# Where the kept weight tiles of a decoder trunk's block products are loaded, and who forms their first sum

## The chip, the cores and the metric

The kernel runs on one core of a Trainium2 chip. The metric is the device time of one execution in microseconds (us). Four compute engines of the core matter here: TensorE (PE in the profile; PEld is its weight load), VectorE (DVE), ScalarE (ACT) and GpSimd (POOL). SyncE (SP) issues the plain loads; POOL issues the accumulating ones. Each engine works through its own list of instructions in order.

## The reference

Two layers of a decoder trunk on 256 positions of width 1024, in float32. Each layer is a half-step feed-forward network (FFN), a token mixer, and a second FFN; the four FFNs are alike. The part that the change touches is the FFN:

```
def swiglu(x, w_in, w_out):
    gate, up = jnp.split(x @ w_in, 2, axis=-1)
    return (jax.nn.silu(gate) * up) @ w_out
...
h = h + 0.5 * swiglu(rms_norm(h, ffn1_norm[l]), ffn1_w_in[l], ffn1_w_out[l])
```

`w_in` is 1024 x 5632 and `w_out` 2816 x 1024. The mixer is a Mamba-2 branch and a gated DeltaNet branch, merged.

## The kernel before, in words

**Weights stream once.** All weights lie in DRAM as tiles of 128 x 1024 float32 (512 KB), in the order of use. A tile is loaded (`load`, L167) and then split on the chip into two float32r halves (`prep`, L180): ScalarE rounds it to `whi` and VectorE subtracts, `wlo = w - whi`. Each product takes three matmuls (`mm3`, `mm3w`, L320 to L332). Raw tiles (`wraw`) have 5 buffers (`NRAW`), the halves 5 pairs (`NSPL`). `take` (L206) hands the next split tile to TensorE and, ahead of that, loads up to `limit` and splits up to 5 forms further on. So a plain load waits on SyncE until VectorE is done with the tile that held its buffer, and a split waits until TensorE is done with the one that held its halves.

**The order of an FFN** is the string `FFN` (L36): one `f` (4 tiles), twenty `c` (2 tiles of `w_in` each, 48 matmuls of 128x256), and in between four `A`; then the close, `BdBBBddddd`. An `A` and its `B` compute one 2x2 block product of `w_out` in Strassen-Winograd form: four weight blocks b11, b12, b21, b22 (two row pairs side by side, 512 KB each) and seven products instead of eight. The weight operands of an `A` are b11, b11+b12, b12+b22 and b11+b12+b22, those of a `B` are b22, b21 and b11+b12+b21+b22. The six `d` tiles are plain rows of `w_out`. The close goes over into the next stage's normalisation: the residual is added to `h`, ScalarE and VectorE normalise, and TensorE transposes the result (`hnT`, L286), first for one half of the positions, then for the other. `join` (L421) adds four combined results to `h` with accumulating transfers.

**A kept tile** (`wsum`, four buffers y0 to y3) carries the sums of one `A` until its `B`. `plan_ffn` (L106) lists the transfers (`stream`) and the forms (`plan`). Two places of `FFN` ahead of each `A` it lists b11 into the kept tile (kind `y`, SyncE) and b12 added onto it by POOL (kind `+`, `add_to`, L164). At the `A` it lists three plain tiles: b12, b22 and again b11. Form `q1` splits the kept b11+b12, and VectorE forms b12+b22 in b12's tile; `q0` splits the plain b11, and VectorE adds b22 onto the kept tile; `q2` splits b12+b22; `q3` splits the kept b11+b12+b22, and then POOL adds b21 onto it (L196), for `q6` in the `B`.

**Who decides the order.** The instructions of one engine are not issued in the order of the source: a scheduler places them by their dependences, and `tc.issue_after` pins one behind another. A plain load waits for one of five buffers. A kept tile has its own buffer, free since the `B` of four groups earlier, and nothing pins its load.

Of the kernel before, what the change touches and what calls it, by code (L numbers as in the profile page):

```python
# [52 lines left out]
def trunk_kernel(ctx, tc, x, wst, wsm, norms, lpar, rpar, cst, out):  # L53
# [15 lines left out]
    def tt(o, a, b, op):  # L69
        return V.tensor_tensor(out=o, in0=a, in1=b, op=op)  # L70
# [15 lines left out]
    def trb(name):  # L86
        return trp.tile([P, 512], F32, tag="tr", name=name)
# [18 lines left out]
    def plan_ffn(j):  # L106


        o, j2, begun, held = j + 4 * FC, j + 4 * FC + 22, [], []
        spots, q = [], 0  # L110
        for at, kind in enumerate(FFN):
            if kind == "A":
                spots.append(at - 2)
        o1 = o + FFN[: FFN.index("A")].count("d")
        for at, kind in enumerate(FFN):
            if at in spots:
                y = len(stream)
                stream.extend([("y", o1 + 4 * q), ("+", o1 + 4 * q + 1, y)])
                begun.append(y)
                q += 1  # L120
            if kind in "fc":
                j = plan_plain(j, 4 if kind == "f" else 2)
            elif kind == "d":
                o = plan_plain(o, 1)
            elif kind == "A":
                y, u = begun.pop(0), len(stream)
                stream.extend([("w", o + 1), ("w", o + 2), ("w", o)])
                plan.append(("q1", (y, u, u + 1), u + 2))
                plan.append(("q0", (u + 2, y, u + 1), u + 3))
                plan.append(("q2", (u,), u + 3))  # L130
                plan.append(("q3", (y, o + 3), u + 3))
                held.append((y, o + 2))
                o += 4
            else:
                y, b22 = held.pop(0)
                stream.append(("w", b22))
                plan.append(("q4", (len(stream) - 1,), len(stream)))
                stream.append(("w", b22 + 1))
                plan.append(("q5", (len(stream) - 1,), len(stream)))
                plan.append(("q6", (y,), len(stream)))  # L140
        return j2
# [19 lines left out]
    def tile_of(i):  # L161
        return wst[i // 2, :, (i % 2) * 1024 :][:, 0:1024]
# [4 lines left out]
    def load(j):  # L167
        kind, i = stream[j][:2]
        if kind == "+":
            add_to(raws[stream[j][2]], i)  # L170
            return
        if kind == "y":
            r = slots.tile([P, 1024], F32, tag=f"y{state['first']}", name="wsum")
            state["first"] = (state["first"] + 1) % 4
        else:
            r = wpool.tile([P, 1024], F32, tag="wraw", name="wraw", bufs=NRAW)
        state["last"] = nc.sync.dma_start(r[:], tile_of(i))
        raws[j] = r

    def prep(i):  # L180
        kind, js, _ = plan[i]
        hi = wpool.tile([P, 1024], F32R, tag="whi", name="whi", bufs=NSPL)
        lo = wpool.tile([P, 1024], F32R, tag="wlo", name="wlo", bufs=NSPL)
        r = raws[js[0]]
        with ExitStack() as behind:
            for ins in state["behind"].pop(i, ()):
                behind.enter_context(tc.issue_after(ins))
            act(hi[:], r[:])
            if kind in ("q0", "q1"):
                to, by = (raws[k][:] for k in js[1:])  # L190
                tt(to, to, by, ALU.add)
            if i in state["late"]:
                behind.enter_context(tc.issue_after(state["late"].pop(i).ins))
            tt(lo[:], r[:], f(hi[:]), ALU.subtract)
        if kind == "q3":
            add_to(r, js[1])  # L196
        for k in {"q0": (js[0], js[-1]), "q1": (), "q3": ()}.get(kind, (js[0],)):
            raws.pop(k)
        halves[i] = (hi, lo)

# [265 lines left out]
    def ffn(nxt):  # L466
        gh = [slots.tile([P, 8, S], F32R, tag=t_, name="gh") for t_ in ("sA", "sB", "sC")]
        gl = [slots.tile([P, 8, S], F32R, tag=t_, name="gl") for t_ in ("sD", "sE", "sF")]

        bsa = slots.tile([P, 2, 2, 3, P], F32R, tag="sG", name="bsa")  # L470
        bsb = slots.tile([P, 16, P], F32R, tag="sH", name="bsb")
        bsc = slots.tile([P, 4, 2, P], F32R, tag="sI", name="bsc")
        bsd = s2.tile([P, 2, 2, P], F32R, tag="s2", name="bsd")
        bsb3 = bsb[:, 0:12].rearrange("p (i o j) t -> p i o j t", i=2, o=2)
        bsb1 = bsb[:, 12:16].rearrange("p (i o) t -> p i o t", i=2)

        def sums(p, j):

            q, i = (p - 1) // 2, (p - 1) % 2
            if j < 3:  # L480
                b = (bsa[:], bsb3)[q % 2]
                return b[:, i, 0, j, :], b[:, i, 1, j, :]
            b = (bsc[:, 0:2], bsc[:, 2:4], bsb1, bsd[:])[q]
            return b[:, i, 0, :], b[:, i, 1, :]

        def block_sums(p, g2):

            sf = tmp2("sf")
            a11, a21, a12, a22 = (g2[:, j * P : (j + 1) * P] for j in range(4))
# [24 lines left out]
        tok_chunk(ps, range(KT))  # L514
        gt = []
        for t in range(2):
            sg = tmp2("sg")
            act(sg[:, 0:256], ps[t][:, 0:256], AF.Silu)
            tt(sg[:, 256:512], sg[:, 0:256], ps[t][:, 256:512], ALU.mult)
            gt.append(sg[:, 256:512])  # L520
        todo, pb, n, cut = FFN[1:], {}, 0, False
        for c in range(FC - 1):
            g2 = tmp2("g2")
            for a in range(2):
                ps = accb("fc")
                chan_chunk(ps, cut or (c, a) == (1, 0))
                cut = False
                sg = s2.tile([P, S], F32, tag="ca", name="sg", bufs=2)
                act(sg[:], ps[:, 0:S], AF.Silu)
                tt(g2[:, a * S : (a + 1) * S], sg[:], ps[:, S : 2 * S], ALU.mult)  # L530
                todo = todo[1:]
                if c == 0 and a == 0:
                    bank = trb("gT")
                    for k in range(2):
                        for t in range(2):
                            PE.transpose(bank[:, k * S + t * P : k * S + (t + 1) * P], gt[t][:, k * P : (k + 1) * P], ident)
                    split(0, bank[:].rearrange("p (k t) -> p k t", k=2))
            split(2 * c + 2, g2[:].rearrange("p (k t) -> p k t", k=2))
            if c + 1 <= PAIRS[-1][-1]:
                block_sums(c + 1, g2)  # L540
            if todo[0] == "A":
                if not pb:
                    pb.update({i: trb(f"p{i}") for i in (5, 6, 1, 7)})
                four = [
                    (pb[5], lambda p: sums(p, 0), PAIRS[n]),
                    (pb[1], lambda p: stat(2 * p, 0), PAIRS[n]),
                    (pb[7], lambda p: sums(p, 2), PAIRS[n]),
                    (pb[6], lambda p: sums(p, 1), PAIRS[n]),
                ]
                block_products(four, n == 0, n == len(PAIRS) - 1)  # L550
                todo, cut = todo[1:], True
                n += 1
        po = [[accb("o"), accb("o")] for _ in range(2)]

        return close_blocks(po, stat, sums, pb, nxt)
# [841 lines left out]
```

## Time and profile before

| what | us |
|---|---|
| median of 3 runs (lowest, highest) | 1556.36 (1554.48, 1556.77) |
| the profiled execution | 1555.2 |
| its span, first to last instruction | 1553.4 |
| TensorE busy in it | 1529.5 |
| VectorE busy | 1210.0 |
| ScalarE busy | 945.9 |
| GpSimd busy | 100.7 |

The page names groups by line, engine, operation and tile. Times within the span count from its start. A matmul's busy time overlaps the next one's, so the distance from one start to the next says how fast TensorE goes: in the FFN's `c` stages 0.11 us from one 128x256 matmul to the next, in the close 0.23 us from one 128x512 matmul to the next. The rows that carry the argument stand in the prediction.

### The profile page before, as it was taken

The numbers are of one execution on the slowest core, as the hardware profiler recorded it, in microseconds if no ns is written. First come the engines' busy times: TensorE is split into PE (matmuls) and PEld (weight loads), VectorE is DVE, ScalarE is ACT, GpSimd is POOL, SyncE is SP. The second block draws the span as 40 slices with busy tenths as digits, with TensorE's granted clock in tenths as the row PEclk, the third lists the DMA queues.
The fourth block names the chain that finished last, engine by engine and source line by source line (L and its number), as shares of the span: only waits on it lengthen the run. The fifth ranks groups of instructions, "written<-read, shape, count | busy, mean of one in ns | idle before, by whom it ended". The sixth has DMA issues, their size and how long they took to land.

```text
span 1553.4 us, 29029 instructions
## 1 busy us (share of the span) xinstructions
PE 1529.5 (98%) x11458; PEld 1384.0 (89%) x11458; DVE 1210.0 (78%) x1840; ACT 945.9 (61%) x1534; POOL 100.7 (6%) x108
## 2 busy tenths in 40 slices
PE   8999999999999999999899999999999999999998
PEld 7999889999888888999689998899998888889996
DVE  6778768967899766878677787699579996677786
ACT  5555677765576545655455566676756665455564
POOL 0000110000000000000100011000000000000010
PEclk9999999999999999999999999999999999999999
DMA  8878775653564686678967787666446557856785
GB/s 292 262 244 261 229 224 165 190 158 109 192 202 163 212 239 200 180 241 248 313 199 209 219 258 231 206 187 187 124 126 213 178 165 223 245 179 199 226 250 156
DMA packets 103439, 322.50 MB, mean 208 GB/s; under 512 B 23350, under 2 KB 24326, under 8 KB 102279
## 3 DMA queue, kind: packets, MB, share of 16 engines
q1 hardware_dynamic: 96390, 299.68, 58.4%
q0 software_dynamic: 6912, 20.97, 8.0%
q8 instruction: 90, 1.47, 0.4%
q14 instruction: 47, 0.38, 0.1%
HBM read 314.50 MB, written 1.92 MB: 204 GB/s over the span
## 4 chain that ended last, share of the span: by engine, by line
PE 82%; DVE 6%; DMA 4%; issue 3%; ACT 3%; POOL 1%; SPq 0%; POOLq 0%; ACTq 0%; DVEq 0%
PE fc L332 9%; PE fc L326 9%; PE fc L331 9%; PE t L321 3%; PE t L322 3%; PE t L323 3%; DMA wraw<-in_wst_dram 3%; PE b L323 3%; PE b L321 3%; PE b L322 3%; PE o L323 2%; PE o L322 2%; PE o L321 2%; DVE wlo L70 2%; PE p L322 2%
## 5 line engine op out<-in xcount | busy, mean ns | idle before, releaser
L70 DVE TENSOR_TENSOR wlo<-wraw,whi 128x1024 fp32r<-128x1024 f32 x504 | 611.2, 1220 | 171.6 <-ACT whi L67 159.9
L67 ACT ACTIVATE whi<-wraw 128x1024 fp32r<-128x1024 f32 x504 | 527.7, 1058 | 275.8 <-PE fc L331 76.6
L332 PE MATMUL fc<-uW,wlo 128*128 128x256 f32 x1280 | 354.8, 277 | 0.0
L326 PE MATMUL fc<-uW,whi 128*128 128x256 f32 x1280 | 354.1, 277 | 0.0
L331 PE MATMUL fc<-uW,whi 128*128 128x256 f32 x1260 | 348.2, 276 | 0.0
L326 PEld LDWEIGHTS fc<-uW,whi 128*128 128x128 f32 x1280 | 240.3, 188 | 0.8
L332 PEld LDWEIGHTS fc<-uW,wlo 128*128 128x128 f32 x1280 | 240.5, 188 | 0.0
L331 PEld LDWEIGHTS fc<-uW,whi 128*128 128x128 f32 x1260 | 236.5, 188 | 0.8
L321 PE MATMUL t<-whi,uW 128*128 128x512 f32 x256 | 101.9, 399 | 0.0
L322 PE MATMUL t<-wlo,uW 128*128 128x512 f32 x256 | 100.9, 394 | 0.0
L323 PE MATMUL t<-whi,uW 128*128 128x512 f32 x256 | 100.6, 393 | 0.0
L321 PE MATMUL b<-whi,bh 128*128 128x512 f32 x192 | 76.2, 398 | 0.3 <-ACT bh L67 0.2
L322 PE MATMUL b<-wlo,bh 128*128 128x512 f32 x192 | 75.0, 390 | 0.0
L323 PE MATMUL b<-whi,bl 128*128 128x512 f32 x192 | 74.3, 394 | 0.3 <-DVE bl L70 0.3
L326 PE MATMUL xs<-uW,whi 128*128 128x256 f32 x256 | 72.7, 284 | 0.0
L332 PE MATMUL xs<-uW,wlo 128*128 128x256 f32 x256 | 71.3, 278 | 0.0
L331 PE MATMUL xs<-uW,whi 128*128 128x256 f32 x254 | 70.5, 277 | 0.0
L67 ACT ACTIVATE whi<-wsum 128x1024 fp32r<-128x1024 f32 x48 | 50.8, 1058 | 27.8 <-PE fc L331 23.3
L70 DVE TENSOR_TENSOR wlo<-wsum,whi 128x1024 fp32r<-128x1024 f32 x48 | 58.6, 1221 | 11.4 <-ACT whi L67 10.4
L322 PE MATMUL o<-wlo,gh 128*128 128x512 f32 x160 | 63.9, 399 | 2.5 <-DVE wlo L70 2.5
L321 PE MATMUL o<-whi,gh 128*128 128x512 f32 x160 | 63.9, 399 | 2.4 <-ACT whi L67 2.4
L165 POOL DMA_DIRECT2D wsum<-in_wst_dram x32 | 28.1, 878 | 582.3 <-DVE wlo L70 464.4
(332 smaller groups left out, 3430.4 us busy)
## 6 DMA issues: line engine op xcount, KB each, us to landing
wraw<-in_wst_dram SPq DMA_DIRECT2D x520, 512.0 KB, 5.0
wsum<-in_wst_dram POOLq DMA_DIRECT2D x32, 512.0 KB, 8.2
wsum<-in_wst_dram SPq DMA_DIRECT2D x16, 512.0 KB, 7.9
dc<-rdram SPq DMA_DIRECT2D x8, 1024.0 KB, 8.4
nw<-in_norms_dram SPq DMA_DIRECT2D x6, 512.0 KB, 6.8
h<-u POOLq DMA_DIRECT2D x12, 256.0 KB, 8.0
gb<-rdram SPq DMA_DIRECT2D x8, 256.0 KB, 5.7
h<-in_x_dram SPq DMA_DIRECT2D x4, 256.0 KB, 3.2
```

Of the source, the lines that this page charges most:

```text
L67: return A.activation(out=o, in_=i, func=func, **kw)
L70: return V.tensor_tensor(out=o, in0=a, in1=b, op=op)
L165: G.dma_start(out=r[:], in_=tile_of(i), accum_op=ALU.add)
L321: PE.matmul(ps, lh, rh, start=start, stop=False)
L322: PE.matmul(ps, lh, rl, start=False, stop=False)
L323: return PE.matmul(ps, ll, rh, start=False, stop=stop)
L326: PE.matmul(ps, wh, mh, start=start, stop=False)
L331: PE.matmul(ps, wh, ml, start=False, stop=False)
L332: PE.matmul(ps, wl, mh, start=False, stop=stop)
```

## The change

Three things change. The kept tile's b11 is listed at its `A`, no longer two places ahead, and its load is issued behind the load listed ahead of it (`issue_after`). b11 is loaded once, into the kept tile only, and VectorE forms b11+b12 there from the plain b12; the accumulating transfer of b12 is gone. The forms come in the order b11, b11+b12, b12+b22, b11+b12+b22 (`q0`, `q1`, `q2`, `q3`), and so do the four products and their result banks (`pb`). Accumulating transfers still form the sum of all four blocks.

Per `A`: SyncE's loads go from four (b11, b12, b22, b11) to three, POOL's accumulating ones from two (b12, b21) to one (b21), VectorE's 128x1024 sums from two to three. There are 16 `A`.

```diff
             elif kind == "A":
-                y, u = begun.pop(0), len(stream)
-                stream.extend([("w", o + 1), ("w", o + 2), ("w", o)])
-                plan.append(("q1", (y, u, u + 1), u + 2))
-                plan.append(("q0", (u + 2, y, u + 1), u + 3))
-                plan.append(("q2", (u,), u + 3))
-                plan.append(("q3", (y, o + 3), u + 3))
+                y = len(stream)
+                stream.extend([("y", o), ("w", o + 1), ("w", o + 2)])
+                plan.append(("q0", (y, y, y + 1), y + 2))
+                plan.append(("q1", (y, y + 1, y + 2), y + 3))
+                plan.append(("q2", (y + 1, y, y + 2), y + 3))
+                plan.append(("q3", (y, o + 3), y + 3))
...
-        state["last"] = nc.sync.dma_start(r[:], tile_of(i))
+        with ExitStack() as behind:
+            if kind != "w":
+                behind.enter_context(tc.issue_after(state["last"].ins))
+            state["last"] = nc.sync.dma_start(r[:], tile_of(i))
...
-            if kind in ("q0", "q1"):
+            if kind in ("q1", "q2"):
                 to, by = (raws[k][:] for k in js[1:])
                 tt(to, to, by, ALU.add)
...
-        if kind == "q3":
+        if kind == "q0":
+            tt(r[:], r[:], raws[js[2]][:], ALU.add)
+        elif kind == "q3":
             add_to(r, js[1])
...
-                    pb.update({i: trb(f"p{i}") for i in (5, 6, 1, 7)})
+                    pb.update({i: trb(f"p{i}") for i in (1, 6, 5, 7)})
                 four = [
+                    (pb[1], lambda p: stat(2 * p, 0), PAIRS[n]),
                     (pb[5], lambda p: sums(p, 0), PAIRS[n]),
-                    (pb[1], lambda p: stat(2 * p, 0), PAIRS[n]),
```

Two places show how this moves instructions. The first is SyncE's list in the close of layer 0's second FFN, whose next stage is layer 1's first FFN; `wraw` are plain tiles and `wsum` kept ones, with the program's running numbers. Before, the four kept tiles of the next FFN stand there, among the last plain loads:

```order
L177 DMA wsum_9035<-in_wst_dram 128x1024
L177 DMA wraw_8546<-in_wst_dram 128x1024
L177 DMA wraw_8558<-in_wst_dram 128x1024
L177 DMA wraw_8580<-in_wst_dram 128x1024
L177 DMA wsum_9398<-in_wst_dram 128x1024
L177 DMA wraw_8598<-in_wst_dram 128x1024
L177 DMA wraw_8620<-in_wst_dram 128x1024
L177 DMA wsum_9735<-in_wst_dram 128x1024
L177 DMA wraw_8642<-in_wst_dram 128x1024
L177 DMA wraw_8664<-in_wst_dram 128x1024
L177 DMA wsum_9983<-in_wst_dram 128x1024
```

After the change, the same list without the running numbers, from the last plain loads ahead of this FFN's own fourth kept tile on; `nw` is a norm's weights:

```order
L170 DMA wraw<-in_wst_dram 128x1024 x6
L170 DMA wsum<-in_wst_dram 128x1024
L170 DMA wraw<-in_wst_dram 128x1024 x29
L214 DMA nw<-in_norms_dram 128x1024
L170 DMA wraw<-in_wst_dram 128x1024 x11
```

The 29 plain loads are the rest of this FFN and the first tiles of the next, with no kept tile among them; the next kept tile follows behind the last row's 11 plain loads. POOL's list moves likewise: between this close's last accumulating transfer onto `h` and the next normalisation stood four accumulating loads of b12 (L165), and now none.

The second place is VectorE's list at the first `A` of layer 0's second FFN. `wraw_7231` and `wraw_7237` are b12 and b22 before; `g2`, `gl` and `sf` belong to the FFN's activations. Before, from the split of an earlier `c` tile on:

```order
L70 TENSOR_TENSOR wlo_7240<-wraw_7096,whi_7239 128x1024
L70 TENSOR_TENSOR wraw_7231<-wraw_7231,wraw_7237 128x1024
L70 TENSOR_TENSOR g2_7229<-sg_7291,fc_7230 128x256
L70 TENSOR_TENSOR wlo_7298<-wraw_7155,whi_7297 128x1024
L70 TENSOR_TENSOR sf_7360<-g2_7229 128x128
L70 TENSOR_TENSOR wlo_7304<-wraw_7161,whi_7303 128x1024
L70 TENSOR_TENSOR wlo_7376<-wsum_7019,whi_7375 128x1024
L70 TENSOR_TENSOR g2_7229<-sg_7355,fc_7294 128x256
L70 TENSOR_TENSOR wsum_7019<-wsum_7019,wraw_7237 128x1024
```

After, where `wraw_7222` and `wraw_7228` are b12 and b22 and `wsum_7152` is the kept tile, from the split of the last `c` tile ahead of the group on:

```order
L70 TENSOR_TENSOR wlo_7295<-wraw_7150,whi_7294 128x1024
L70 TENSOR_TENSOR wlo_7365<-wsum_7152,whi_7364 128x1024
L70 TENSOR_TENSOR g2_7220<-sg_7346,fc_7285 128x256
L70 TENSOR_TENSOR wsum_7152<-wsum_7152,wraw_7222 128x1024
L70 TENSOR_TENSOR gl_6835<-g2_7220,gh_6832 128x512
L70 TENSOR_TENSOR sf_7351<-g2_7220 128x128
L70 TENSOR_TENSOR wraw_7222<-wraw_7222,wraw_7228 128x1024
L70 TENSOR_TENSOR sf_7351<-sf_7351,g2_7220 128x128
L70 TENSOR_TENSOR wlo_7372<-wsum_7152,whi_7371 128x1024
L70 TENSOR_TENSOR sf_7351<-g2_7220,sf_7351 128x128
L70 TENSOR_TENSOR wsum_7152<-wsum_7152,wraw_7228 128x1024
```

The sum b12+b22 stood ahead of two splits of `c` tiles and of all splits of its group; it now stands behind the first split of the group and behind the new sum b11+b12. The group has three sums instead of two.

More of the change, by code (lines that the diff above doesn't have):

```diff
@@ L106, in plan_ffn @@
     def plan_ffn(j):
[L109 to L120, printed above, removed]
+        o, j2, held = j + 4 * FC, j + 4 * FC + 22, []
+        for kind in FFN:
             if kind in "fc":
@@ L194, in prep @@
             tt(lo[:], r[:], f(hi[:]), ALU.subtract)
-        if kind == "q3":
+        if kind == "q0":
+            tt(r[:], r[:], raws[js[2]][:], ALU.add)
+        elif kind == "q3":
             add_to(r, js[1])
-        for k in {"q0": (js[0], js[-1]), "q1": (), "q3": ()}.get(kind, (js[0],)):
+        for k in {"q0": (), "q1": (), "q2": js[::2], "q3": ()}.get(kind, (js[0],)):
             raws.pop(k)
```

## The prediction

> **What bounds the kernel now.** The page comes first: how much of the span is TensorE, and what the chain that ended last consists of.
>
> ```profile
> span 1553.4 us, 29029 instructions
> PE 1529.5 (98%) x11458; PEld 1384.0 (89%) x11458; DVE 1210.0 (78%) x1840; ACT 945.9 (61%) x1534; POOL 100.7 (6%) x108
> ...
> PE 82%; DVE 6%; DMA 4%; issue 3%; ACT 3%; POOL 1%; SPq 0%; POOLq 0%; ACTq 0%; DVEq 0%
> ```
>
> TensorE is busy for 1529.5 of 1553.4 us, and none of its matmuls is removed. So the change can only win where TensorE waits or is slowed, and lose where it would begin to wait. To find such a place I compare like with like: the four FFNs do the same work, and each begins with the same transposes. The chain, in order of time, has them (start, duration, what), and two long transfers between:
>
> ```profile
> 16.97 0.63 PE hnT L286 x4
> ...
> 195.10 0.66 PE hnT L286 x4
> ...
> 601.23 0.63 PE hnT L286 x4
> ...
> 744.30 8.13 DMA wraw<-in_wst_dram
> ...
> 755.17 12.27 DMA wraw<-in_wst_dram
> ...
> 788.56 0.66 PE hnT L286 x4
> ...
> 966.44 0.66 PE hnT L286 x4
> ```
>
> From start to start, layer 0's first FFN takes 195.10 - 16.97 = 178.13 us, layer 1's first 966.44 - 788.56 = 177.88 us, but layer 0's second 788.56 - 601.23 = 187.33 us. It is 9.2 to 9.45 us longer, and it alone has loads of weights of 8 and 12 us in the chain. The last FFN ends the program and has no such successor. The table by stretches tells where the excess lies: the rows begin at the same point of the close in each of the three FFNs and end at the transposes (us, then busy time of each engine with its instructions, granted TensorE clock, DMA share, GB/s).
>
> ```profile
> core 0: us, PE busy (x) PEld busy (x) DVE busy (x) ACT busy (x) POOL busy (x), PEclk, DMA share, GB/s
> 157.10:195.10 38.00, 37.62 (x170) 30.87 (x169) 30.13 (x34) 24.22 (x31) 4.84 (x6) 1.00 0.75 226
> 741.20:788.60 47.40, 42.26 (x172) 32.39 (x170) 30.45 (x35) 24.14 (x31) 7.83 (x9) 0.93 0.91 278
> 928.40:966.40 38.00, 37.69 (x170) 30.88 (x169) 29.58 (x33) 24.38 (x31) 4.15 (x5) 1.00 0.74 223
> ```
>
> The same 170 matmuls take 47.4 us instead of 38.0: all of the excess is in this close, at a DMA share of 0.91 against 0.75 and a clock of 0.93 against 1.00. The DMA view of the close names the transfers (KB each, median us to landing): here four lines of layer 0's second FFN, then the plain loads of layer 1's first.
>
> ```profile
> wraw<-in_wst_dram SPq DMA_DIRECT2D x13, 512.0 KB, 10.8
> wsum<-in_wst_dram SPq DMA_DIRECT2D x4, 512.0 KB, 10.6
> wsum<-in_wst_dram POOLq DMA_DIRECT2D x4, 512.0 KB, 8.8
> ```
>
> ```profile
> wraw<-in_wst_dram SPq DMA_DIRECT2D x12, 512.0 KB, 6.0
> ```
>
> Eight transfers of 512 KB belong to kept tiles of the next FFN, and beside them a plain load takes 10.8 us, where it takes 6.0 without them. The close uses up a split tile every 1.36 us (six matmuls, below) and has five buffers, so a load has some 6.8 us from one use of its buffer to the next: 6.0 fits, 10.8 doesn't. TensorE's rows show the result, first an undisturbed step, then the last tiles:
>
> ```profile
> 758.05 0.39 PE L321 MATMUL o<-whi,gh 128*128 128x512 f32 x1
> 758.28 0.39 PE L322 MATMUL o<-wlo,gh 128*128 128x512 f32 x1
> ...
> 766.53 0.39 PE L323 MATMUL o<-whi,gl 128*128 128x512 f32 x1
> 768.65 0.80 PE L321 MATMUL o<-whi,gh 128*128 128x512 f32 x1 [1.73 <-ACT whi L67]
> 769.91 0.80 PE L322 MATMUL o<-wlo,gh 128*128 128x512 f32 x1 [0.46 <-DVE wlo L70]
> 770.50 0.63 PE L323 MATMUL o<-whi,gl 128*128 128x512 f32 x1
> 770.93 0.63 PE L321 MATMUL o<-whi,gh 128*128 128x512 f32 x1
> ...
> 774.77 0.43 PE L321 MATMUL o<-whi,gh 128*128 128x512 f32 x1
> ```
>
> ```profile
> 768.00:775.00 7.00, 5.88 (x13) 4.32 (x14) 1.92 (x2) 1.32 (x3) 0.86 (x1) 0.51 1.04 352
> ```
>
> TensorE waits for the splits, the splits for the loads; then, from 768 to 775 us, the granted clock is 0.51 and a step takes 0.43 us instead of 0.23. From 769.91 to 774.77 us that costs half of 4.86, 2.4 us; the other 6.9 of the 9.3 us are waits.
>
> **The change, part by part.**
>
> *Kept tiles leave this close.* SyncE's new list has no kept tile among this close's loads, and POOL's none of the four accumulating ones. What remains is what the closes at 157 and 928 us have, with the same four transfers onto `h`. Value taken: 38.0 us as there, so -9.3 us, slow clock included. Bounds: 0 (something else makes the loads slow) and -9.45.
>
> [...]
>
> *Transfers removed.* Per `A` one plain and one accumulating load go, 32 in all. In the closes at 157 and 928 us TensorE is busy for 37.6 and 37.7 of 38.0 us without this relief, so 0 is taken for it elsewhere, with up to 1 us of gain for small waits on loads that the rows above do not show.
>
> *Sixteen more sums on VectorE.* A sum is measured:
>
> ```profile
> L70 DVE TENSOR_TENSOR wsum<-wsum,wraw x16: 1215/1218/1226, 65.4 to 1491.8; 128x1024 f32<-128x1024 f32 x16
> ```
>
> 16 x 1.218 = 19.5 us of VectorE. Whether TensorE sees it depends on room in each cycle from one `A` to the next:
>
> ```profile
> 123.70:140.20 16.50, 16.50 (x124) 15.55 (x123) 15.06 (x21) 10.65 (x15) 0.88 (x1) 1.00 0.78 237
> ...
> 653.20:680.50 27.30, 27.30 (x219) 26.35 (x218) 21.87 (x32) 16.16 (x22) 0.89 (x1) 1.00 0.75 224
> ...
> 707.90:724.40 16.50, 16.50 (x123) 15.55 (x123) 13.88 (x18) 10.11 (x13) 0.86 (x1) 1.00 0.75 219
> ```
>
> In a long cycle VectorE goes from 21.9 to 23.1 of 27.3 us, in the short one (two `c`) from 13.9 to 15.1 of 16.5. The tightest short cycle, 15.06, would come to 16.3 of 16.5. But VectorE also loses time to late loads, and this goes, because the sum b12+b22 no longer stands ahead of other splits in VectorE's list:
>
> ```profile
> DVE wraw L70 <- DMA wraw<-in_wst_dram: 39.0, 16, 6.1
> ```
>
> Sixteen waits, 39.0 us, against 19.5 us of new work. Then there is the order within a group: its sums and splits are now one chain on the kept tile. Of the first `A` of layer 0's second FFN, the first and last split, and TensorE's first use of these two:
>
> ```profile
> 643.68 1.23 DVE L70 TENSOR_TENSOR wlo<-wsum,whi 128x1024 fp32r<-128x1024 f32 x1 [0.18 <-ACT whi L67]
> ...
> 653.15 1.22 DVE L70 TENSOR_TENSOR wlo<-wsum,whi 128x1024 fp32r<-128x1024 f32 x1 [1.85 <-ACT whi L67]
> ```
>
> ```profile
> 653.56 0.40 PE L322 MATMUL p<-wlo,bsa 128*128 128x512 f32 x1
> ...
> 657.65 0.39 PE L322 MATMUL p<-wlo,bsa 128*128 128x512 f32 x1
> ```
>
> The last split ends at 654.37 and is used at 657.65: 3.3 us in hand. VectorE idles for 1.85 us before it, more than a sum's 1.22; even if all of the 1.22 showed, 2.1 us would be left. So 0 is taken. If the cover were gone, each group would cost up to 1.22 us: bounds 0 and +19.5, 0 being the nearer by these rows. ScalarE's second rounding of a group now waits for VectorE's first sum, and the activations queued behind it wait too; they feed later stages, under the same cover.
>
> *The kept tile's load comes late.* It has its own buffer, so it waits only behind the plain load ahead of it, and that load waits for its buffer. Its landing is measured on the page:
>
> ```profile
> wsum<-in_wst_dram SPq DMA_DIRECT2D x16, 512.0 KB, 7.9
> ```
>
> The first split of a group ends at 644.91 and is used at 653.56, 8.65 us later. A load listed one place ahead has the 6.8 us of the buffers at the least, and the first split may be 8.65 us late before TensorE waits: 7.9 us fit. Value 0; if not, at most 7.9 - 6.8 = 1.1 us each, inside the 19.5 above.
>
> *Order of products and banks.* The same four products in another order, ended by the same bank: 0.
>
> The sum: -9.3 us. The profiled execution, 1555.2 us (its span plus 1.8), becomes 1545.9. The median of the runs is 1.16 us above that execution, and the same step from 1556.36 gives **1547.1 us**.
>
> **The rivals.**
>
> *Only part of the close is repaired* (0.08). The four transfers onto `h` are issued in the same close, and loads may still be too slow. For it: DMA is at 0.75 even in the good closes. Against it: those two closes have the same transfers and take 38.0 us. With half of the excess left, 1556.4 - 4.65 = 1551.7.
>
> *The slow clock stays* (0.03): the waits go, but the 2.4 us at half clock have another cause and come again in this close or the next, 1556.4 - 6.9 = 1549.5. For it: the idle time ahead of the drop is 1.73 us only. Against it: the clock is 1.00 in the two closes without waits. [...]
>
> *The kept tiles are not the cause* (0.04): the next FFN's first loads are what fills the queues. Then nothing goes: 1556.4. Against it: the plain loads landed 4.8 us later exactly beside the kept ones.
>
> *VectorE becomes the bound in the sixteen groups* (0.06). It decides from the point where the chain of a group exceeds the 3.3 us in hand, in the short cycles first, where room is 1.4 us. Then every group costs up to 1.22 us: 1547.1 + 19.5 = 1566.6, slower than before. Against it: the 39.0 us of waiting that go, and 1.85 us idle in the middle of the chain.
>
> **How the numbers follow.** The forecast has 0.79: 1547.1, from 1545 (another 1 us gained and the runs' own scatter) to 1549. The range reaches to the half-repaired close: 1544.6 to 1551.7. What is left out is a close that stays as it is and a VectorE bound, some 0.10, and a little on either side of the forecast. About 0.2%, 3.1 us, is what a measurement of this kernel can tell from no change: faster 0.90 (forecast, partial repair, slow clock), same 0.04, slower 0.06.
>
> **What would show it.** Right: the stretch from this close's first `B` to the transposes takes 38 us, its clock is 1.00, plain loads land in about 6 us, and the chain has no load of 8 us there; the FFN from transposes to transposes takes 178 us. VectorE's waits for loads in front of `wraw<-wraw` fall far below 39.0 us while its busy time rises by some 19 us. Wrong: TensorE's rows on `p` show waits for `wlo`, or the clock in the groups falls below 1.00, or the close keeps waits above 2 us.

## The result, and the profile after

The changed kernel takes 1547.4 us (median of 6 runs, 1545.78 to 1549.02), beside 1556.57 us for the kernel before on the same chip (6 runs, 1553.76 to 1559.66). The ratio is 0.9941, with a 95% interval from 0.9927 to 0.9956: faster by 0.6%. The forecast was 1547.1 us.

The page of the changed kernel: span, busy times, the two data queues (packets, MB, share of 16 engines' time) and the shares of the chain that ended last.

```profile
span 1546.4 us, 29049 instructions
PE 1525.9 (99%) x11458; PEld 1383.8 (89%) x11458; DVE 1228.8 (79%) x1856; ACT 949.3 (61%) x1534; POOL 86.9 (6%) x92
...
q1 hardware_dynamic: 94086, 291.29, 55.9%
q0 software_dynamic: 4608, 12.58, 4.9%
...
PE 86%; DVE 5%; issue 3%; ACT 3%; DMA 2%; POOL 1%; POOLq 0%; SPq 0%; ACTq 0%; DVEq 0%
```

The profiled execution took 1548.12 us, its span plus 1.7. DMA's share of the chain has fallen from 4% to 2%. The starts of the FFNs' transposes tell where the time came from; the chain, in order of time:

```profile
16.45 0.63 PE hnT L281 x4
...
194.69 0.66 PE hnT L281 x4
...
602.93 0.63 PE hnT L281 x4
...
780.96 0.66 PE hnT L281 x4
...
959.02 0.65 PE hnT L281 x4
```

The three FFNs that have a successor take 194.69 - 16.45 = 178.24, 780.96 - 602.93 = 178.03 and 959.02 - 780.96 = 178.06 us. Layer 0's second FFN is no longer the odd one (187.33 us before). Its close, in the table by stretches, between the closes of its neighbours (the columns are those of the tables above):

```profile
156.70:194.70 38.00, 37.65 (x171) 30.88 (x169) 29.58 (x33) 24.32 (x31) 4.18 (x5) 1.00 0.74 225
743.00:781.00 38.00, 37.61 (x171) 30.88 (x169) 30.41 (x34) 24.20 (x31) 4.19 (x5) 1.00 0.76 232
921.00:959.00 38.00, 37.64 (x170) 30.86 (x168) 29.59 (x33) 24.35 (x31) 4.15 (x5) 1.00 0.73 223
```

All three rows read alike: 38.00 us, clock 1.00, a DMA share of about three quarters. 47.40 us had become 38.00. The DMA issues from 730 to 764 us hold no kept tile, and a plain load lands after 6.3 us instead of 10.8:

```profile
wraw<-in_wst_dram SPq DMA_DIRECT2D x17, 512.0 KB, 6.3
```

The FFN gave back 187.33 - 178.03 = 9.30 us and the medians of the runs differ by 9.2 us, but the two profiled executions differ by 7.1 us only (1555.2 and 1548.12). The rest lies in the first mixer: from the transposes at 194.69 us to those at 602.93 us it takes 408.24 us, and took 601.23 - 195.10 = 406.13 us before. A second profile of each kernel, below, shows that this is scatter.

### The profile page after: what moved, and what is told of

Same layout as the page of the kernel before. It is cut to its first block, busy times and chain, and to the rows that moved or that the text cites. A ratio compares the mean times of both kernels' runs of the same rounds, so it can differ in the third digit from the quotient of the medians.

```text
span 1546.4 us, 29049 instructions
## 1 busy us (share of the span) xinstructions
PE 1525.9 (99%) x11458; PEld 1383.8 (89%) x11458; DVE 1228.8 (79%) x1856; ACT 949.3 (61%) x1534; POOL 86.9 (6%) x92
## 4 chain that ended last, share of the span: by engine, by line
PE 86%; DVE 5%; issue 3%; ACT 3%; DMA 2%; POOL 1%; POOLq 0%; SPq 0%; ACTq 0%; DVEq 0%
PE fc L327 9%; PE fc L321 9%; PE fc L326 9%; PE o L318 3%; PE o L317 3%; PE o L316 3%; PE t L316 3%; PE t L317 3%; PE t L318 3%; PE b L318 3%; PE b L316 3%; PE b L317 3%; PE p L317 2%; PE p L316 2%; PE p L318 2%
## 5 line engine op out<-in xcount | busy, mean ns | idle before, releaser
L70 DVE TENSOR_TENSOR wlo<-wraw,whi 128x1024 fp32r<-128x1024 f32 x488 | 592.2, 1221 | 188.1 <-ACT whi L67 174.5
L67 ACT ACTIVATE whi<-wraw 128x1024 fp32r<-128x1024 f32 x488 | 511.6, 1059 | 268.1 <-PE fc L326 91.6
L67 ACT ACTIVATE whi<-wsum 128x1024 fp32r<-128x1024 f32 x64 | 68.0, 1062 | 58.8 <-PE fc L326 32.7
L70 DVE TENSOR_TENSOR wlo<-wsum,whi 128x1024 fp32r<-128x1024 f32 x64 | 78.2, 1222 | 7.9 <-ACT whi L67 5.6
L318 PE MATMUL o<-whi,gl 128*128 128x512 f32 x160 | 62.3, 389 | 0.0
```

The costliest lines, as they stand in the source:

```text
L67: return A.activation(out=o, in_=i, func=func, **kw)
L318: return PE.matmul(ps, ll, rh, start=False, stop=stop)
```

## The experiments

Three measures serve throughout. *FFN* is the time from transposes to transposes in layer 0's second FFN. *Close* is the time from the start of the first to the start of the last matmul on `gh` in the close, from the timeline of TensorE: 41.03 us before, 31.72 after, and 30.8 to 31.8 in FFNs that nothing disturbs. *Stages ahead* is the time from an FFN's first matmul onto `f` to the first matmul of its close (the first onto `o`), for the four FFNs in turn: 147.23, 144.49, 144.33 and 144.50 us before, 147.04, 144.49, 144.52 and 144.30 after.

**The theory** was the prediction's: the eight transfers for kept tiles slow the close's loads, and getting them out of this close is the whole gain. **Its rivals**: it is not eight transfers alike, but the accumulating ones among them; or the new order of the loads costs something that the rest of the change pays back; or VectorE is at its limit.

### e1_pin_only: the new order of the loads, without the new sums

In the kernel before, each kept load is issued behind the preceding load, as in the changed kernel. The tile is still loaded twice, and b12 is still accumulated onto the kept tile by POOL.

```diff
-        state["last"] = nc.sync.dma_start(r[:], tile_of(i))
+        with ExitStack() as behind:
+            if kind != "w":
+                behind.enter_context(tc.issue_after(state["last"].ins))
+            state["last"] = nc.sync.dma_start(r[:], tile_of(i))
```

> The kernel before with one line of the change: each kept tile's load is issued behind the load listed ahead of it; b12 is still added onto it by an accumulating transfer, and b11 is still loaded twice. Theory (the kept tiles' transfers in the close of layer 0's second FFN cost 9.3 us): they leave that close, the FFN from transposes to transposes takes 178 us as the others, and the whole comes to 1546 to 1549 us, faster than before by 8 to 10 us. Rival (the gain comes from the smaller traffic and from the sum on VectorE): the time stays within 3 us of before, 1553 to 1559 us, and the close still takes over 44 us.

Measured: 1567.88 us (6 runs, 1563.36 to 1569.57) beside 1557.30 us (17 runs); ratio 1.0058 (1.0042 to 1.0075), slower. The close was indeed repaired: 32.13 us. But the stages ahead took 149.13, 151.39, 146.34 and 151.13 us, 2 to 7 us more in each FFN. Neither theory had expected that, and the whole is slower than both forecasts. The waits between 690 and 716 us, a stage with groups of sums (us in all, times, longest):

```profile
POOL wsum L165 <- DMA wsum<-in_wst_dram: 46.5, 2, 31.3
...
DVE wraw L70 <- DMA wraw<-in_wst_dram: 8.5, 1, 8.5
...
PE fc L335 <- DVE wlo L70: 3.1, 1, 3.1
```

And the two rows that join them, of VectorE and of TensorE:

```profile
706.58 1.23 DVE L70 TENSOR_TENSOR wraw<-wraw 128x1024 f32<-128x1024 f32 x1 [8.50 <-DMA wraw<-in_wst_dram]
```

```profile
709.32 0.58 PE L335 MATMUL fc<-uW,wlo 128*128 128x256 f32 x1 [3.08 <-DVE wlo L70]
```

VectorE stands 8.50 us at the sum b12+b22, which waits for a load; the splits of `c` tiles behind it in its list come late, and TensorE waits 3.08 us for one of them. A second suspect is POOL's row: its accumulating transfer waits for the kept load to land (31.3 us at the longest), so that two transfers in a row now lie between the late issue and the group's first split. The next two experiments are for this question.

### e9_pin_plain: is it the two in a row, or the accumulating?

e1_pin_only, with POOL's transfer plain instead of accumulating. It still has to wait for the kept load, whose tile it writes.

```diff
-            add_to(raws[stream[j][2]], i)
+            G.dma_start(out=raws[stream[j][2]][:], in_=tile_of(i))
             return
```

> The kernel of e1_pin_only (before, with every kept load issued behind the preceding load), but b12 is a plain transfer on POOL instead of an accumulating one; the kept tile then holds b12 alone, and the sum b11+b12 is left out. The transfer on POOL still has to wait until the kept load has landed, since it writes the same tile. Theory series: the stalls of 2 to 7 us in the A stages come from two transfers in a row ahead of the group's split, whatever the second one does; then from the FFN's start to its close there are 146 to 151 us as in e1_pin_only, and the time is 1558 to 1568. Rival: the accumulating transfer itself is what is too slow; then 144.3 to 145 us from start to close (147 in the first FFN), closes of 31.7 us, and 1546 to 1550.

Measured: 1561.62 us (10 runs, 1557.2 to 1564.07) beside 1556.51 us (13 runs); ratio 1.0031 (1.0017 to 1.0044). The stages ahead took 148.13, 148.72, 146.51 and 147.10 us, the close 32.99 us (the other FFNs' 31.97 to 32.89). So the stalls stay when the second transfer is plain. They are shorter: over the undisturbed stages (147.1 and 144.4 us) 10 us in the four FFNs, where e1_pin_only has 17.7. But part of that difference is the clock: from 690 to 716 us it was 0.87 on the average in e1_pin_only, 1.00 in this kernel, and over the whole profiled executions 0.995 and 0.998, which by an estimate (0.003 of 1560 us) is some 4.7 us. By its expectation this run speaks for the pair in a row; the next one shows that this reading is wrong.

### e10_pin_late_sum and e11_late_sum: where VectorE's sum stands

e1_pin_only and the kernel before, each with the sum b12+b22 behind the first split of its group on VectorE, as the changed kernel has it. All transfers stay, the accumulating ones too, and no sum is added.

```diff
-            if kind in ("q0", "q1"):
+            if kind == "q0":
                 to, by = (raws[k][:] for k in js[1:])
                 tt(to, to, by, ALU.add)
...
-            tt(lo[:], r[:], f(hi[:]), ALU.subtract)
+            split = tt(lo[:], r[:], f(hi[:]), ALU.subtract)
+        if kind == "q1":
+            to, by = (raws[k][:] for k in js[1:])
+            with tc.issue_after(split.ins):
+                tt(to, to, by, ALU.add)
```

> The kernel of e1_pin_only, with one thing more: VectorE's sum b12+b22 stands behind the first split of its group, as in the changed kernel, and no longer ahead of splits of c tiles. The kept tile is still loaded late and b12 accumulated onto it. Theory VectorE order: TensorE's waits in the stages ahead came from VectorE standing at that sum; then from the FFN's start to its close there are 147 to 147.5 us in the first and 144.3 to 145 us in the other FFNs, no drop of the clock in them, closes of 31 to 32 us, and 1546 to 1550 us. Rival late pair: the two transfers in a row make the kept tile itself late; then TensorE waits for splits of the kept tile, the stages ahead still take 146 to 151 us, and the time is 1555 to 1568.

> The kernel before with VectorE's sum b12+b22 behind the first split of its group, and nothing else; the kept loads come early, as before. Both theories: the sum's waits of 39 us on VectorE fall far below that, but its waits had cost TensorE nothing, so that the stages ahead stay at 147 and 144.4 us; the close of layer 0's second FFN still has its eight transfers and takes 38 to 42 us, and the time is 1554 to 1559, as that of the kernel before. If the time falls by more than 3 us, the order on VectorE was a cause of its own.

Measured, both beside 1556.88 us (13 runs): with the pin 1548.75 us (4 runs, 1545.82 to 1549.93), ratio 0.9944 (0.9928 to 0.9961); without it 1555.13 us (10 runs, 1554.09 to 1556.75), ratio 0.9989 (0.9979 to 0.9998). With the pin the stages ahead take 146.90, 144.30, 144.46 and 144.32 us and all closes 31.75 us or less: the whole loss of e1_pin_only is gone and the whole gain of the change is there. The stretch that had stalled, and the waits of the whole run:

```profile
690.00:716.00 26.00, 26.00 (x207) 25.05 (x206) 21.61 (x32) 16.37 (x22) 1.72 (x2) 1.00 0.98 282
```

```profile
POOL wsum L165 <- DMA wsum<-in_wst_dram: 326.2, 13, 32.8
...
DVE wraw L70 <- DMA wraw<-in_wst_dram: 2.1, 3, 0.9
```

POOL's accumulating transfers still wait up to 32.8 us for the kept loads, and among the waits of the run no matmul waits for a split of a weight tile: the two in a row were harmless. VectorE's waits at the sum have gone from 68.9 us (e1_pin_only) to 2.1; in e9_pin_plain, where the sum stood in its old place too, they were 65.7. The place of one sum in VectorE's list, with the loads late, was the cause. Without the pin the same move is worth 1.7 us (0.3 to 3.3 by the interval), and the close is about as slow as ever. Its stretch, and its plain loads:

```profile
742.00:789.40 47.40, 43.03 (x179) 33.45 (x178) 30.45 (x34) 24.89 (x32) 7.62 (x9) 0.93 0.91 276
```

```profile
wraw<-in_wst_dram SPq DMA_DIRECT2D x14, 512.0 KB, 9.6
```

### e2_no_pin: the new sums, without the new order of the loads

The changed kernel with the kept loads issued as early as their buffers allow, so that the next FFN's four come into the close again; no accumulating ones come with them.

```diff
-        with ExitStack() as behind:
-            if kind != "w":
-                behind.enter_context(tc.issue_after(state["last"].ins))
-            state["last"] = nc.sync.dma_start(r[:], tile_of(i))
+        state["last"] = nc.sync.dma_start(r[:], tile_of(i))
```

> The changed kernel without the pin: b11 is loaded once and the sum b11+b12 is made on VectorE, but a kept tile's load may be issued as early as its buffer is free, so four loads of 512 KB (not the four accumulating ones) are again among the last loads of layer 0's second FFN. Theory: about half of the extra traffic is back in the close, so 2 to 6 us of the 9.3 come back, 1549 to 1554 us, and plain loads there land in 7 to 9 us. Rival (the gain comes from smaller traffic and the sum on VectorE): 1546 to 1549 us as the changed kernel.

Measured: 1548.68 us (5 runs, 1548.16 to 1549.78) beside 1557.30 us; ratio 0.9941 (0.9926 to 0.9956), the same as that of the whole change. The theory, which wanted 2 to 6 us back, was wrong: the median shows none of it, and in the profile the close is 1.2 us longer. The close's row, and its DMA issues from 730 to 770 us:

```profile
743.00:782.30 39.30, 38.41 (x172) 30.87 (x170) 30.16 (x34) 24.24 (x31) 4.20 (x5) 1.00 0.82 278
```

```profile
wraw<-in_wst_dram SPq DMA_DIRECT2D x17, 512.0 KB, 6.7
wsum<-in_wst_dram SPq DMA_DIRECT2D x4, 512.0 KB, 7.2
```

Four plain kept loads in the close move a plain load from 6.3 to 6.7 us, which is still within the 6.8 us in which a buffer comes round (an estimate: five buffers, one tile used up every 1.36 us), and the close (first to last matmul) from 31.72 to 32.90 us. The clock stays at 1.00.

### e8_plain_plus: eight transfers, none of them accumulating

The kernel before, with POOL's four transfers plain; the diff is that of e9_pin_plain.

> The kernel before, with b12's accumulating transfer onto each kept tile turned into a plain one of the same size, from the same queue, at the same place: the kept tile then holds b12 in place of b11+b12, so that sum is left out of what is computed. Theory A (it is the accumulating that is dear: the software queue's packets take 8.0% of the engines' time for 20.97 MB, the plain queue's 58.4% for 299.68 MB, twice as much per byte): the close of layer 0's second FFN, 41.0 us from its first to its last matmul on gh before and 31.7 undisturbed, comes down to 33 to 37 us, the whole to 1548 to 1553 us. Theory B (eight transfers of 512 KB are too many, of whatever kind): 39 to 41 us and 1555 to 1559 us.

Measured: 1553.13 us (6 runs, 1551.4 to 1555.02) beside 1557.19 us (13 runs); ratio 0.9975 (0.9964 to 0.9987). Close 36.29 us, FFN 182.6 us. The stretch of the close, the DMA issues from 734 to 774 us, and the two queues on the page:

```profile
741.60:784.40 42.80, 40.26 (x173) 31.95 (x171) 29.81 (x33) 24.50 (x31) 5.68 (x8) 0.96 0.87 302
```

```profile
wraw<-in_wst_dram SPq DMA_DIRECT2D x13, 512.0 KB, 8.5
wsum<-in_wst_dram SPq DMA_DIRECT2D x4, 512.0 KB, 8.0
wsum<-in_wst_dram POOLq DMA_DIRECT2D x4, 512.0 KB, 8.1
```

```profile
q1 hardware_dynamic: 96390, 299.68, 59.0%
q0 software_dynamic: 6912, 20.97, 6.6%
```

Close and time agree with theory A (the time is 0.13 us above its range). The same bytes at the same place; only the accumulation is gone, and about half of the close's excess with it. With e2_no_pin this makes a ladder for one close (landing times of the loads issued in some 30 to 40 us around it):

| kept transfers in the close | plain load lands after | close |
|---|---|---|
| none (changed kernel) | 6.3 us | 31.72 us |
| none, moved behind (e10_pin_late_sum) | 5.8 us | 31.75 us |
| 4 plain (e2_no_pin) | 6.7 us | 32.90 us |
| 4 plain on SyncE, 4 plain on POOL (e8_plain_plus) | 8.5 us | 36.29 us |
| 4 plain, 4 accumulating (kernel before) | 10.8 us | 41.03 us |

Below the 6.8 us of a buffer's round little more than 1 us was lost; above it, each further microsecond of landing cost the close some 2 us on the average of these rows. Of the excess of 9.3 us, making the four transfers accumulating is 4.7 us, their being there at all 3.4, and the four plain kept loads 1.2. The first of these is the least certain: two other profiles with the transfers of the last row have a close of 39.44 us (e7_before_again) and one of 40.15, with a landing of 9.6 us (e11_late_sum), which leaves 3.2 to 4.7 us for the accumulating.

### e3_pin_third: the new order of the loads in one FFN alone

The kernel before, with only the four kept loads of layer 1's first FFN, those that fell into the slow close, behind the preceding load.

```diff
+            if kind == "y":
+                state["kept"] = state.get("kept", 0) + 1
+                if 8 < state["kept"] <= 12:
+                    behind.enter_context(tc.issue_after(state["last"].ins))
```

> The kernel before, with the pin for the four kept tiles of layer 1's first FFN alone; the other twelve are issued as before. Theory (one close carries the whole loss): the same gain as with all sixteen pinned, 1546 to 1549 us. Rival (each of the four FFNs gains a part): a quarter of the gain, 1553 to 1556 us.

Measured: 1552.77 us (12 runs, 1549.87 to 1555.92) beside 1557.30 us; ratio 0.9969 (0.9957 to 0.9982), between the two forecasts. Close 31.82 us, FFN 178.1 us: the transfers taken out of it are the cause of all its excess, and nothing else is. But the FFN to which the four tiles belong pays with 148.65 us ahead of its close instead of 144.4. TensorE's wait there, and two stretches of 3.4 us, the one with the wait and the one behind it:

```profile
886.10 0.38 PE L337 MATMUL fc<-uW,wlo 128*128 128x256 f32 x1 [2.16 <-DVE wlo L70]
```

```profile
883.40:886.80 3.40, 1.24 (x11) 1.05 (x11) 3.40 (x5) 0.00 (x0) 0.53 (x1) 1.00 0.24 96
...
886.70:890.20 3.50, 3.50 (x20) 3.50 (x19) 3.50 (x5) 1.32 (x2) 0.44 (x1) 0.51 0.83 160
```

One wait of 2.16 us was followed by 3.4 us at half clock, in which TensorE was busy without a gap: by an estimate, half of those 3.4 us, the wait costs about 1.7 us more than itself.

### e4_more_1 and e4_more_3: how much room VectorE has left

The changed kernel with the group's second split done again, once or three times more: 16 or 48 further operations of 1.22 us.

```diff
             tt(lo[:], r[:], f(hi[:]), ALU.subtract)
+            if kind == "q1":
+                for _ in range(1):
+                    tt(lo[:], r[:], f(hi[:]), ALU.subtract)
```

> The changed kernel with one more VectorE operation of 1.22 us in each of the sixteen groups (the subtraction for the half of b11+b12 is made twice, to the same result), 19.5 us of VectorE in all. If the groups have room for it (3.3 us in hand less the 1.22 us of the change leave 2.1): 1546 to 1549 us, as the changed kernel. Rival (VectorE already is the bound after the change): 16 x 1.22 = 19.5 us more, 1562 to 1568 us.

> The changed kernel with three more VectorE operations of 1.22 us in each of the sixteen groups, 3.66 us a group. The room of 2.1 us is then used up: up to 1.6 us a group show, 10 to 35 us in all with the halved clock that follows on waits, 1558 to 1583 us. Rival (the room is much larger than the rows say): 1546 to 1550 us.

Measured, both beside 1557.19 us: 1548.46 us with one more (4 runs, 1547.92 to 1552.37; ratio 0.9951, 0.9938 to 0.9963), which can't be told from the changed kernel's ratio; and 1593.61 us with three more (4 runs, 1589.67 to 1595.42; ratio 1.0227, 1.0212 to 1.0242). A short cycle with one more, then a long one with three more, each from its kernel, and the waits of the latter:

```profile
702.40:718.90 16.50, 16.50 (x124) 15.55 (x123) 16.50 (x26) 10.96 (x16) 0.86 (x1) 1.00 0.58 165
```

```profile
655.30:685.00 29.70, 28.10 (x215) 26.30 (x214) 26.12 (x37) 15.55 (x22) 0.93 (x1) 1.00 0.56 174
```

```profile
PE p L320 <- DVE wlo L70: 13.6, 16, 1.6
...
PE fc L330 <- DVE wlo L70: 9.0, 12, 0.8
```

With one more, VectorE is busy for all 16.50 us of the short cycle and TensorE still has no gap in it. With three more, the time is above the expected 1558 to 1583 us: 58.6 us of work cost some 46 us of time, 2.9 us a group; TensorE's matmuls on `p`, those of the groups, wait for `wlo` sixteen times. So the cover ends between one and three operations more, and the rival mechanism of VectorE as the bound is real, with its point just beyond this kernel.

### e5_no_accum: the last sum on VectorE too

The changed kernel with b21 added on VectorE from the load that the close makes anyway, instead of POOL's accumulating transfer.

```diff
-                plan.append(("q3", (y, o + 3), y + 3))
+                plan.append(("q3", (y,), y + 3))
...
-                plan.append(("q5", (len(stream) - 1,), len(stream)))
+                plan.append(("q5", (len(stream) - 1, y), len(stream)))
...
-        elif kind == "q3":
-            add_to(r, js[1])
+        elif kind == "q5":
+            tt(raws[js[1]][:], raws[js[1]][:], r[:], ALU.add)
```

> The changed kernel with the fourth sum on VectorE too: b21 is added onto the kept tile from the plain load of b21 that the close makes anyway, so no accumulating transfer of weights and 16 loads fewer; VectorE gets 16 sums of 1.22 us, four in each close. If TensorE waits for nothing in the closes: 1546 to 1549 us, no change. If VectorE binds there (three splits and a sum, 4.9 us, for a B whose matmuls take 4.1): up to 0.8 us for each of the 16 B, 1548 to 1560 us.

Measured: 1566.27 us (6 runs, 1562.72 to 1571.87) beside 1557.19 us; ratio 1.0063 (1.0045 to 1.0082). All four closes suffer, 37.67, 35.69, 38.02 and 37.55 us. The first of them, then two waits of the whole run:

```profile
156.50:200.60 44.10, 40.98 (x172) 31.81 (x171) 33.83 (x39) 24.38 (x31) 5.47 (x6) 0.96 0.66 202
```

```profile
PE o L317 <- DVE wlo L70: 7.0, 13, 0.9
...
PE o L316 <- ACT whi L67: 4.7, 3, 1.7
```

This is dearer than either expectation. DMA is idler than before (0.66), and TensorE waits for splits: the likely reason is that in the close a sum lies in the chain from a load to its use, which has no slack. A rival was not tried: VectorE stood for 19.5 us at its sums onto kept tiles until a load had landed (13 waits, all at the four closes), so that here, too, the place of the sum in its list may count. Either way the same operation was free in a group (e4_more_1) and dear in a close.

### e7_before_again and e6_after_again: second profiles

The kernel before and the changed kernel, each once more.

> The kernel before once more, unchanged, for a second profile. Theory: layer 0's second FFN again takes 187 us from transposes to transposes, with the clock halved for some 7 us, and the two mixers (406.1 and 406.6 us in the first profile, 408.2 and 408.1 in the changed kernel's) scatter by 1 to 2 us between profiles of one kernel. Rival (the change makes the mixers slower by 2 us each): they take 406.1 and 406.6 us again, within 0.5 us.

> The changed kernel once more, for a second profile. If its close is repaired for good, layer 0's second FFN takes 178 us again and its close 31.7 us from the first to the last matmul on gh, with no drop of the clock; the mixers may differ by up to 3 us from the first profile, as they do between two profiles of the kernel before. Rival (one profile was lucky): a close of over 33 us or a stretch at half clock.

The kernel before took 1559.65 us, its close 39.44 us with 6.8 us at half clock, the FFN 185.6 us; the two mixers, counted from transposes to transposes, took 408.5 and 409.0 us. The changed kernel took 1546.97 us, its close 31.72 us with no drop of the clock, the FFN 178.0 us. The close of the second profile of the changed kernel:

```profile
743.40:781.40 38.00, 37.64 (x170) 30.87 (x168) 30.00 (x34) 24.02 (x31) 4.22 (x5) 1.00 0.78 233
```

The slow close comes again in the one and the repair in the other. The mixer of 406.13 us lies within the scatter of one kernel.

## Why the prediction was right

**The bound and the place.** "All of the excess is in this close" held: 47.40 us became 38.00, and the FFN 187.33 became 178.03. e3_pin_third shows it without the rest of the change.

**Kept tiles leave this close, -9.3 us.** Shown in place, and in size to about 2 us: the median fell by 9.2 us, but in its second profile the kernel before has only 185.6 us in this FFN, 7.6 more than the changed kernel. That forecast and median agree to 0.3 us is in part luck. What the step had not seen is that its eight transfers are not eight alike, and that either of two parts of the change would have done: with the accumulating ones gone, the early kept loads cost 1.2 us in the close and nothing that the medians show (e2_no_pin); with all transfers kept but issued late, and VectorE's sum in its new place, the gain is the same 0.6% (e10_pin_late_sum).

**The slow clock goes, 2.4 of the 9.3 us.** The rival that it stays is refuted here: no drop from 13 to 1542 us in the changed kernel. That the clock can drop behind idle times of no more than 1.73 us is borne out: in e8_plain_plus it did so behind gaps of 0.63 and 0.76 us,

```profile
763.49 0.50 PE L321 MATMUL o<-whi,gh 128*128 128x512 f32 x1 [0.63 <-ACT whi L67]
764.75 0.50 PE L322 MATMUL o<-wlo,gh 128*128 128x512 f32 x1 [0.76 <-DVE wlo L70]
...
766.67 0.80 PE L322 MATMUL o<-wlo,gh 128*128 128x512 f32 x1 [0.76 <-DVE wlo L70]
```

though e4_more_3, whose matmuls on `p` waited up to 1.6 us for splits, has a mean clock of 0.999, as the changed kernel has. So the longest gap did not decide it in these runs. The last heading goes further into it.

**Transfers removed, 0 to -1 us elsewhere.** The queues carry 8.39 MB less each, and the stages ahead of the closes, 147.04 to 144.30 us, stand within 0.2 us of those before. 0 was right.

**Sixteen more sums on VectorE, 0.** Its busy time rose by 1228.8 - 1210.0 = 18.8 us, where 19.5 was worked out, and its waits for plain loads fell as foreseen. The row for VectorE's waits, then the sums' group, which now counts 32:

```profile
DVE wraw L70 <- DMA wraw<-in_wst_dram: 1.1, 2, 0.7
```

```profile
L70 DVE TENSOR_TENSOR wsum<-wsum,wraw x32: 1215/1219/1227, 60.6 to 1488.6; 128x1024 f32<-128x1024 f32 x32
```

39.0 us have become 1.1. The prediction took this for relief that pays for the new sums. It is more: in the kernel before, these waits cost little (1.7 us, e11_late_sum), but with the kept loads late they go with 17.7 us of loss ahead of the closes (e1_pin_only, 68.9 us of them). The new sums themselves buy nothing that e10_pin_late_sum, without them, doesn't have. The occupancy of the cycles, long and short, from the same points of the FFN as the prediction's rows at 653.20 and 707.90 us:

```profile
654.90:682.20 27.30, 27.30 (x219) 26.35 (x218) 22.91 (x34) 16.26 (x22) 0.93 (x1) 1.00 0.72 231
...
709.60:726.10 16.50, 16.50 (x123) 15.55 (x123) 15.56 (x20) 9.16 (x12) 0.86 (x1) 1.00 0.81 247
```

Both are near what was foreseen (23.1 foreseen, 22.91 measured; 15.1 and 15.56). The tightest one, at 123.70 us, was to come to 16.3 and came to 15.44 (123.50 to 140.00 us). But the room in a short cycle depends on where its row is cut: 7.4 us earlier, the first FFN's row reads 16.43 of 16.50 us before the change (116.30 to 132.80 us) and 16.40 after (116.10 to 132.60). So a full row alone is no sign of a bound: TensorE is busy for all 16.50 us of each of these rows.

**The chain within a group** (3.3 us in hand before, at least 2.1 left). The first and last split of the first group in layer 0's second FFN, and TensorE's first use of these two:

```profile
645.38 1.23 DVE L70 TENSOR_TENSOR wlo<-wsum,whi 128x1024 fp32r<-128x1024 f32 x1 [0.18 <-ACT whi L67]
...
654.95 1.22 DVE L70 TENSOR_TENSOR wlo<-wsum,whi 128x1024 fp32r<-128x1024 f32 x1
```

```profile
655.27 0.40 PE L317 MATMUL p<-wlo,gh 128*128 128x512 f32 x1
...
659.36 0.39 PE L317 MATMUL p<-wlo,bsa 128*128 128x512 f32 x1
```

The last split ends at 656.17 and is used at 659.36: 3.2 us in hand, so the new sum has filled idle time, as the 1.85 us of idling ahead of the split had suggested. But the slack of the last split is not the room of the group: three operations more, 3.66 us, cost 2.9 us a group, not 3.66 - 3.2 = 0.5.

**The kept tile's load comes late, 0.** 0 was right, and for the reason given: the tile itself is in time, even with a second transfer behind its load (e10_pin_late_sum). What the step missed is the cost of the same delay to another instruction, VectorE's early sum; it is 0 only because the change moves that sum too. **The order of products, 0**, was not tried by itself, though e10_pin_late_sum has the old order and the same time.

What stays open: why VectorE's waits at the early sum grow from 39.0 to 68.9 us with the pin. The chain of e1_pin_only shows one of these loads issued when its buffer came free and landing after 9.55 us, beside a kept load and an accumulating transfer; with that transfer plain the waits are still 65.7 us (e9_pin_plain), and no run takes only that traffic away.

## What to carry to other kernels

A transfer that is issued as soon as its buffer is free can land in a stage that has no room for it, as the eight for kept tiles did here: compare the landing time of that stage's loads with the time in which its buffers come round. In this close extra traffic was nearly free below that (6.7 of 6.8 us, +1.2 us) and was paid above it (8.5 us, +4.6 us; 10.8 us, +9.3 us). When loads are moved later, look in every engine's list for an instruction that waits for them ahead of work that is due sooner: here one sum in the wrong place turned a gain of 9 us into a loss of 10, and moving it made even the two transfers in a row harmless. Look also at the stage to which an operation is added: one more of 1.22 us on VectorE was free in the sixteen groups (0 us), where VectorE had idle time (22.91 of 27.30 us busy in a long cycle, 15.56 of 16.50 in a short one), and four of them were dear in each close (4 to 7 us), where TensorE then waited for splits.

## What the runs showed of the hardware

**Accumulating transfers took about twice as much of the engines' time per byte.** On the page of the kernel before, the software queue took 8.0% of the engines' time for 20.97 MB and the plain queue 58.4% for 299.68 MB: 0.38% and 0.195% per MB. With b12's transfers plain and b21's still accumulating (e8_plain_plus), the software queue's share falls to 6.6% for the same 20.97 MB. The 8.39 MB made plain thus take 1.4% less, 0.17% less per MB, which leaves 0.21% per MB for them, close to the plain queue's 0.195%.

**The clock fell behind steps of 3.4 us in which TensorE was idle for nearly half the time or more, also without a long gap.** In seven profiles (the kernel before, e1_pin_only, e3_pin_third, e5_no_accum, e7_before_again, e8_plain_plus, e11_late_sum) rows show one drop in the middle of the run, of about 3.4 or 6.8 us, and in the 3.4 us just ahead of it TensorE was busy for 1.06 to 1.79 us only. The stretch ahead of the drop in the kernel before, then the one of e8_plain_plus, where no gap was longer than 0.76 us:

```profile
764.60:768.00 3.40, 1.23 (x3) 0.48 (x3) 1.23 (x1) 0.74 (x2) 0.00 (x0) 1.00 1.05 284
```

```profile
762.80:766.20 3.40, 1.72 (x5) 0.67 (x4) 2.04 (x2) 1.70 (x2) 0.00 (x0) 1.00 1.02 406
```

Such busy time does not decide it alone. Two steps behind which the clock stayed at 1.00, of the changed kernel, then of the kernel before, just ahead of its row above:

```profile
405.80:409.20 3.40, 1.77 (x9) 1.41 (x9) 3.37 (x7) 0.96 (x3) 0.00 (x0) 1.00 0.49 201
```

```profile
761.20:764.60 3.40, 2.08 (x6) 0.86 (x6) 2.33 (x2) 1.84 (x2) 0.86 (x1) 1.00 1.05 363
```

By TensorE's busy time the two kinds of row overlap: 1.77 us without a drop and, in e7_before_again from 766.50 to 769.90 us, 1.79 ahead of one. By the busy time of its weight loads they overlap as well: 0.86 us without a drop, but 1.05 us in e3_pin_third's step ahead of one. What decides it stays open: the steps ahead of these drops were not wholly idle.
